# Seven blocks instead of eight in the second layer's mixture of experts

## The chip, the cores and the metric

The program runs on one core of one Trainium2 chip. The metric is the device time of one execution in microseconds (us), as the median of three runs. An execution takes about a thousandth of a second. In this text TensorE is called PE and its weight loads PEld, VectorE is DVE, ScalarE is ACT, GpSimd is POOL, and SyncE, whose queue issues most of the transfers, is SP.

## What is computed

Two layers over 256 latent tokens and 256 context tokens, width 1024, all in float32. Each layer has a mixer (attention) and a mixture of 16 experts, of which each token uses two. The change lies in the second layer's mixture, where only the 256 latent tokens are left. It is this much of the reference:

```python
expert_id = g_idx[:, None] * EXPERTS_PER_GROUP + top_i
dense_gate = jnp.einsum('nk,nke->en', weights, jax.nn.one_hot(expert_id, N_EXPERTS, dtype=jnp.float32))

def expert_step(acc, params):
    wg, wu, wd, gate = params
    y = (jax.nn.silu(tok @ wg) * (tok @ wu)) @ wd
    return acc + gate[:, None].astype(y.dtype) * y, None

out, _ = lax.scan(expert_step, jnp.zeros_like(tok), (w_gate, w_up, w_down, dense_gate))
```

`wg` and `wu` are 1024 x 512, `wd` is 512 x 1024: 6 MiB for an expert, 96 MiB for the layer. After the mixture comes a last RMSNorm.

## The kernel before

The kernel does not compute every expert for every token. It gathers for each expert the tokens that chose it into **slots**, a fixed number for each (`CAPS`, L32). In the second layer the first four experts by number (ranks 12 to 15) have 32 slots each; the other twelve are ranked on the chip by how many tokens chose them, and ranks 0 and 1 have 192 slots, ranks 2 and 3 have 128, ranks 4 to 11 have 32. Tokens that find no slot go through a slow path behind a branch (L1752) that is entered only if there are any.

128 slots make a **block** (`PLAN` L37, `block_plan` L55). Of the second layer's eight blocks, block 0 holds the four experts with known numbers, 32 slots each (a "q" entry); blocks 1 and 2 one expert each, ranks 3 and 2 ("m"); the "w" entry makes three blocks: block 3 with the last 64 slots of ranks 0 and 1, and blocks 4 and 5 with their first 128; blocks 6 and 7 hold ranks 8 to 11 and 4 to 7.

Each block has three products: gate (G), up (U) and down (D). The string `TURNS` (L69) gives their order in the second layer by hand: G6 is the gate product of block 6. The rest of this text names products in that way. In a product, PE holds the block's tokens as weights and streams the expert's matrix through, 512 columns at a time, with one instruction of `T.matmul` for each tile of the block (L1658 for G and U, L1691 for D). Tiles of 32 or 64 slots lie side by side in the array's columns, so that a block of four 32-slot tiles takes four matmuls for what a block of one 128-slot tile does with one. This text calls one such pass of 512 columns a **round**: every product has 8 rounds, whatever its tiles. (The trace shows each matmul as two instructions.)

Around the products, each block costs PE some more work: `pick` (L1326), 48 short matmuls that gather the block's tokens out of three bf16 parts, at kt = 2 of the product ahead of its G; `ready` (L1427, L1430), which lays out the gather matrix and the gates; `a_turn` (L1619), four transposes between U and D; and `ship` with `chunk` (L1589, L1596), which spreads the block's result back over the tokens, eight matmuls put behind later products by `spread_some`.

The weights come in **loads** of 1 MiB (128 partitions x 8 KiB), two for each expert and product: the first half serves rounds 1 to 4, the second rounds 5 to 8. `Experts.todo` (L1003) lists all 96 loads of the layer in the order in which `TURNS` needs them first; this text numbers them 0 to 95. They rotate over 18 buffers (`more["order"]`, L1919), so load n has to wait until the last product that reads load n - 18 is done. All are issued on SP's queue, in order, at most eight under way: an issue that waits holds up all that stand behind it. The matrices of ranks 0 to 11 can be addressed only when the ranking is known; then SP reads each expert's number out of `perm` into a register (`value_load`, L1020) the first time that it is wanted. Loads 0 to 15 are issued earlier; `experts.issue(len(fixed) - 4 + 2 * l)` (L1349) issues what is left of the experts with known numbers ahead of the ranking.

Of the kernel before, what the change touches and what calls it, by code (L numbers as in the profile page):

```python
# [30 lines left out]

CAPS = (  # L32
    (192, 192) + (128,) * 4 + (64,) * 10,
    (192, 192) + (128,) * 2 + (32,) * 12,
)

PLAN = (  # L37
    (("p", 14, 15), ("m", 2), ("p", 12, 13), ("m", 3), ("p", 10, 11), ("w", 0, 1), ("m", 4), ("m", 5), ("p", 8, 9),
     ("p", 6, 7)),
    (("q", 12, 13, 14, 15), ("m", 3), ("m", 2), ("w", 0, 1), ("q", 8, 9, 10, 11), ("q", 4, 5, 6, 7)),  # L40
)
MAXSLOTS = max(sum(c) for c in CAPS)

# [1 line left out]
def bases(layer):  # L45

    out, n = [0] * NE, 0
    for _, *rs in PLAN[layer]:
        for r in rs:
            out[r] = n  # L50
            n += CAPS[layer][r]
    return out


def block_plan(layer):  # L55

    base, blocks = bases(layer), []
    for kind, *rs in PLAN[layer]:
        if kind == "w":
            pair = [(base[r] + 128, 64, r) for r in rs]  # L60
            ones = [[(base[r], 128, r)] for r in rs]
            blocks += [pair] + ones if layer else [ones[0], pair, ones[1]]
        else:
            blocks.append([(base[r], 128 // len(rs), r) for r in rs])
    return blocks

TURNS = ("G0 U0 G1 U1 D0 D1 G6 G4 U6 U4 G3 G5 D6 U3 D4 U5 D3 D5 G7 G2 U2 U7 D2 D7")  # L69


def products(layer):

    if layer:
        return [("GUD".index(t[0]), int(t[1:])) for t in TURNS.split()]
    out, n = [], len(block_plan(layer))
    for b in range(n):
        turn = [(0, b), (1, b)], [(2, b - 1)] * (b > 0)  # L80
        out += turn[1] + turn[0] if b == n - 1 else turn[0] + turn[1]
    return out + [(2, n - 1)]
# [83 lines left out]
def hybrid_kernel(ctx: ExitStack, tc: tile.TileContext, A: dict, dbg=None):  # L166
# [829 lines left out]
    class Experts:  # L996


        def __init__(self, l):
            self.l, self.w, self.regs, self.perm = l, {}, {}, None  # L1000
            blocks = block_plan(l)
            self.known = NE - NFIX[l]
            self.todo = list(dict.fromkeys((r, which, h) for which, b in products(l) for h in range(2)  # L1003
                                           for _, _, r in blocks[b]))
            if l == 0:
                self.todo.sort(key=lambda p: p[0] < self.known)
# [36 lines left out]
    def moe(l, ntb, experts, yp, yT, finish, w_o, place, after_loads):  # L1043
# [214 lines left out]
        fx = tl([ntb, nfix], "fx")  # L1258
        V.scalar_tensor_tensor(fx, pos[:, :, 0:nfix], 1.0, Mb[:, :, 0:nfix], op0=ALU.add, op1=ALU.mult)
        blocks = block_plan(l)  # L1260

        solo = [len(b) == 1 and l in SPLIT for b in blocks]
# [699 lines left out]
```

## Time and profile before

| what | value |
| --- | --- |
| time, median of three runs | 1064.69 us (1059.69 to 1064.75) |
| time of the profiled execution | 1066.53 us |
| its span, first to last instruction | 1064.7 us |
| busy in the span: PE, DVE, ACT | 985.5, 556.2, 397.3 us |
| mean granted clock of TensorE | 0.976 of 2.4 GHz |
| moved by DMA | 309.85 MB, mean 291 GB/s |
| second layer's products, first G0 to the end of D7 | 824.8 to 1049.6 us |

The profile gives busy time by engine, the rate of the DMA, the idle time of each engine with the engine that ended it, and the instructions in order of time. A busy PE can be a PE that waits inside a matmul, so the count of rounds in a stretch is read beside its busy share. The rows that the prediction uses stand below, in groups.

### The profile page before, as it was taken

The numbers are of one execution on the slowest core, as the hardware profiler recorded it, in microseconds if no ns is written. First come the engines' busy times: TensorE is split into PE (matmuls) and PEld (weight loads), VectorE is DVE, ScalarE is ACT, GpSimd is POOL, SyncE is SP. The second block draws the span as 40 slices with busy tenths as digits, with TensorE's granted clock in tenths as the row PEclk, the third lists the DMA queues.
The fourth block names the chain that finished last, engine by engine and source line by source line (L and its number), as shares of the span: only waits on it lengthen the run. The fifth ranks groups of instructions, "written<-read, shape, count | busy, mean of one in ns | idle before, by whom it ended". The sixth has DMA issues, their size and how long they took to land. (4 is left out here: it accounts for less than half of the span.)

```text
span 1064.7 us, 14592 instructions
## 1 busy us (share of the span) xinstructions
PE 985.5 (93%) x5205; PEld 574.6 (54%) x5205; DVE 556.2 (52%) x1354; ACT 397.3 (37%) x817; POOL 49.2 (5%) x73
## 2 busy tenths in 40 slices
PE   4899999897999989999986999998878999999995
PEld 3666555686555435566422668885556444434532
DVE  3564465767565545578325745627877422214324
ACT  4254343643234324567204525327873311100211
POOL 3000100100000000000021000000000000000000
PEclk9999999999999999999989999999998999999998
DMA  9988877536779998989896593333164999999991
GB/s 284 367 332 323 342 312 275 201 136 212 289 312 411 358 422 307 367 332 357 333 383 228 215 398 128 119 119 158 41 220 139 383 420 419 420 374 408 380 374 41
DMA packets 66950, 309.85 MB, mean 291 GB/s; under 512 B 6544, under 2 KB 14944, under 8 KB 37176
## 3 DMA queue, kind: packets, MB, share of 16 engines
q1 hardware_dynamic: 56408, 277.01, 67.0%
q0 software_dynamic: 5984, 19.26, 5.3%
q10 hardware_dynamic: 4480, 12.59, 3.3%
q8 instruction: 43, 0.70, 0.3%
q14 instruction: 35, 0.29, 0.1%
HBM read 299.85 MB, written 8.98 MB: 290 GB/s over the span
## 5 line engine op out<-in xcount | busy, mean ns | idle before, releaser
L1658 PE MATMUL gu<-we,xT 128*64 128x512 f32 (+1 forms) x512 | 119.6, 616 | 3.2 <-DMA we<-in_w_up_dram 3.2
L1691 PE MATMUL dn<-we,aT 128*64 128x512 f32 (+2 forms) x480 | 119.1, 606 | 2.8 <-DMA we<-in_w_down_dram 2.6
L317 ACT CAST wh<-we 128x512 fp32r<-128x512 f32 x144 | 85.5, 621 | 64.1 <-PE dn L322 24.3
L1658 PE MATMUL gu<-we,xt 128*32 128x512 f32 (+2 forms) x448 | 105.2, 596 | 0.0
L318 DVE TENSOR_TENSOR wl<-we,wh 128x512 fp32r<-128x512 f32 x144 | 92.2, 687 | 20.9 <-ACT wh L317 19.2
L321 PE MATMUL mm<-wh,hT 128*128 128x512 f32 x248 | 101.5, 409 | 1.8 <-ACT hT L317 1.8
L322 PE MATMUL mm<-wh,hT 128*128 128x512 f32 x248 | 97.8, 394 | 0.7 <-DVE hT L318 0.7
L323 PE MATMUL mm<-wl,hT 128*128 128x512 f32 x248 | 98.1, 395 | 0.0
L1691 PEld LDWEIGHTS dn<-we,aT 128*64 128x64 f32 (+2 forms) x480 | 36.0, 134 | 66.1 <-issue 59.1
L1658 PEld LDWEIGHTS gu<-we,xT 128*64 128x64 f32 (+1 forms) x512 | 33.7, 133 | 62.3 <-issue 54.6
L1658 PEld LDWEIGHTS gu<-we,xt 128*32 128x32 f32 (+2 forms) x448 | 36.3, 136 | 57.2 <-issue 55.1
L318 DVE TENSOR_TENSOR wl<-wi,wh 128x512 fp32r<-128x512 f32 x52 | 35.7, 690 | 48.3 <-ACT wh L317 34.6
L1669 DVE TENSOR_TENSOR sg<-sg,gu 128x256 f32<-128x256 f32 x40 | 15.2, 417 | 83.8 <-PE gu L1658 80.8
L321 PEld LDWEIGHTS mm<-wh,hT 128*128 128x128 f32 x248 | 46.9, 189 | 20.5 <-issue 8.4
L317 ACT CAST wh<-wi 128x512 fp32r<-128x512 f32 x52 | 32.1, 621 | 64.0 <-PE mm L322 59.6
L323 PEld LDWEIGHTS mm<-wl,hT 128*128 128x128 f32 x248 | 46.9, 189 | 12.2 <-issue 0.8
L322 PEld LDWEIGHTS mm<-wh,hT 128*128 128x128 f32 x248 | 47.0, 189 | 10.6 <-DVE hT L318 1.0
L317 ACT CAST y<-y 128x512 fp32r<-128x512 f32 x16 | 9.9, 618 | 97.6 <-DVE y L1589 85.1
L321 PE MATMUL mm<-wo,yT 128*128 128x512 f32 x96 | 40.9, 426 | 2.3 <-ACT wo L317 2.3
L350 PE MATMUL ada<-wada,cs 128*32 128x512 f32 x320 | 40.8, 600 | 0.5 <-DMA wada<-in_w_ada_dram 0.5
L1664 ACT ACTIVATE sg<-gu 128x512 f32<-128x512 f32 x20 | 11.9, 597 | 77.7 <-PE gu L1658 72.0
L323 PE MATMUL mm<-lo,yT 128*128 128x512 f32 x96 | 39.2, 410 | 1.1 <-DVE lo L318 1.0
(367 smaller groups left out, 1658.0 us busy)
## 6 DMA issues: line engine op xcount, KB each, us to landing
we<-in_w_gate_dram SPq DMA_DIRECT2D x64, 1024.0 KB, 10.3
we<-in_w_up_dram SPq DMA_DIRECT2D x62, 1024.0 KB, 8.7
we<-in_w_down_dram SPq DMA_DIRECT2D x60, 1024.0 KB, 15.9
wada<-in_w_ada_dram SPq DMA_DIRECT2D x48, 1024.0 KB, 8.9
wi<-in_w_in_odd_dram SPq DMA_DIRECT2D x12, 1024.0 KB, 8.9
win<-in_w_in_even_dram SPq DMA_DIRECT2D x4, 1024.0 KB, 11.7
wo<-in_w_out_even_dram SPq DMA_DIRECT2D x4, 1024.0 KB, 8.3
we<-in_w_down_dram ACTq DMA_DIRECT2D x4, 1024.0 KB, 14.7
```

The costliest lines, as they stand in the source:

```text
L317: S.copy(hi, src)
L318: V.tensor_tensor(out=lo, in0=src, in1=hi.bitcast(F32), op=ALU.subtract)
L321: T.matmul(ps, a[0], b[0], start=start, stop=False)
L322: T.matmul(ps, a[1], b[0], start=False, stop=False)
L323: T.matmul(ps, a[0], b[1], start=False, stop=stop)
L350: T.matmul(ps[32 * j:32 * j + 32], cs[:, kt, :], part(w, k)[:, 512 * j:512 * j + 512], start=(kt == 0), stop=(kt == KT - 1))
L1658: T.matmul(ps[c:c + n_], xTs[bi][0][:, kt, c:c + n_], part(experts.w[r, which], kt), start=(kt == 0), stop=(kt == KT - 1))
L1664: S.activation(parted(sgs[bi], 4), by_part(ps, 4), AF.Silu)
L1669: V.tensor_tensor(out=sg[:, c], in0=sg[:, c], in1=up[:, c], op=ALU.mult)
L1691: T.matmul(ps[h][c:c + n_], aTs[bi][0][:, f, c:c + n_], part(experts.w[r, 2], f)[:, 512 * h:512 * h + 512], start=(f == 0), stop=(f == 3))
```

## The change

`CAPS` gives ranks 0 and 1 160 slots in the second layer (192 before) and rank 3 64 (128 before). A new "x" entry takes the place of rank 3's "m" and of the "w" entry. It makes three blocks: ranks 0 and 1 with 128 slots each, and one block of four tiles of 32 slots: the last 32 of rank 0, the last 32 of rank 1, and two tiles of rank 3. Seven blocks are left: 0 (ranks 12 to 15), 1 (rank 2), 2 (rank 0), 3 (rank 1), 4 (the four tiles), 5 (ranks 8 to 11), 6 (ranks 4 to 7). `TURNS` is written anew for them. The branch of "x" for four ranks is not taken here.

```diff
@@ -31,13 +31,14 @@
 CAPS = (
     (192, 192) + (128,) * 4 + (64,) * 10,
-    (192, 192) + (128,) * 2 + (32,) * 12,
+    (160, 160) + (128, 64) + (32,) * 12,
 )
 PLAN = (
     ...
-    (("q", 12, 13, 14, 15), ("m", 3), ("m", 2), ("w", 0, 1), ("q", 8, 9, 10, 11), ("q", 4, 5, 6, 7)),
+    (("q", 12, 13, 14, 15), ("m", 2), ("x", 0, 1, 3), ("q", 8, 9, 10, 11), ("q", 4, 5, 6, 7)),
 )
@@ -60,13 +61,19 @@
+        elif kind == "x":
+            ones = [[(base[r], 128, r)] for r in rs[:2]]
+            tiles = lambda *rs: [(base[r] + n, 32, r) for r in rs for n in range(128 if CAPS[layer][r] > 128 else 0,
+                                                                                CAPS[layer][r], 32)]
+            blocks += ones + [tiles(*rs)] if len(rs) == 3 else [ones[0], tiles(rs[0], rs[2]), ones[1],
+                                                                tiles(rs[1], rs[3])]
         else:
             blocks.append([(base[r], 128 // len(rs), r) for r in rs])
-TURNS = ("G0 U0 G1 U1 D0 D1 G6 G4 U6 U4 G3 G5 D6 U3 D4 U5 D3 D5 G7 G2 U2 U7 D2 D7")
+TURNS = ("G0 U0 D0 G2 U2 G4 U4 D2 G3 U3 D4 D3 G6 U6 G1 G5 U1 D6 U5 D1 D5")
```

The order moves in two places of which the prediction speaks. Lines of the changed kernel stand 7 higher (L1658 is L1665, L1691 is L1698, L1596 is L1603, L1619 is L1626, L1020 is L1027, L216 is L223).

The first is SP's queue where the ranking becomes known. `perm` is the ranking; `we` is a buffer of weights. Before, SP reads one number behind the first sixteen loads and goes on with a gate matrix:

```order
L216 DMA we<-in_w_up_dram 128x2048 x8
L1020 TENSOR_LOAD perm
L1020 ISA x2
L216 ISA
L216 DMA we<-in_w_gate_dram 128x2048
L216 ISA
L216 DMA we<-in_w_gate_dram 128x2048
L216 ISA
L216 DMA we<-in_w_up_dram 128x2048
L216 ISA
L216 DMA we<-in_w_up_dram 128x2048
L216 DMA we<-in_w_down_dram 128x2048 x8
```

In the changed kernel two of block 0's eight down loads stand ahead of the first read:

```order
L223 DMA we<-in_w_gate_dram 128x2048 x8
L223 DMA we<-in_w_up_dram 128x2048 x8
L223 DMA we<-in_w_down_dram 128x2048 x2
L1027 TENSOR_LOAD perm
L1027 ISA x2
```

Ten reads follow in a row; the last two of them, and what stands behind:

```order
L1027 TENSOR_LOAD perm
L1027 ISA x2
L1027 TENSOR_LOAD perm
L1027 ISA x2
L223 DMA we<-in_w_down_dram 128x2048 x6
L223 ISA
L223 DMA we<-in_w_gate_dram 128x2048
```

What moved: block 0's down loads go from places 20 to 27 of the list to places 16 to 23, and ten reads of the ranks, of which one stood there and the others singly between later loads, stand in front of load 18.

The second is the end of PE's program. `gu` and `dn` are the products' sums, `xt` the gathered tokens, `aT` the turned activations, `sp` the spreading. Before, from U2 on (U2, U7, D2, the start of D7):

```order
L1658 MATMUL gu<-we,xt 128x512 x8
L1658 MATMUL gu<-we,xt 32x512 x16
L1619 MATMUL tr<-cst,sg 128x128 x4
L1658 MATMUL gu<-we,xt 32x512 x16
L1691 MATMUL dn<-we,aT 128x512 x4
L1619 MATMUL tr<-cst,sg 128x128 x4
L1691 MATMUL dn<-we,aT 128x512 x4
L1691 MATMUL dn<-we,aT 32x512 x2
```

In the changed kernel, from U5 on (the rest of U5, D1, the start of D5):

```order
L1665 MATMUL gu<-we,xt 32x512 x31
L1698 MATMUL dn<-we,aT 128x512 x4
L1626 MATMUL tr<-cst,sg 128x128 x4
L1698 MATMUL dn<-we,aT 128x512 x4
L1698 MATMUL dn<-we,aT 32x512 x2
```

The last three products are now U5, D1 and D5, which need 18 loads that no earlier product reads; before they were U7, D2 and D7, which needed 18 as well, behind G7, G2 and U2 with 12. What follows the last D is the same list of instructions in both.

## Rows read from the trace of the kernel before

**Rows 1.** Page, part 2: rate of the DMA in 40 slices of 26.6 us.

```profile
GB/s 284 367 332 323 342 312 275 201 136 212 289 312 411 358 422 307 367 332 357 333 383 228 215 398 128 119 119 158 41 220 139 383 420 419 420 374 408 380 374 41
```

**Rows 2.** Stretches of the second mixture: busy us (count) by engine, PE's clock, DMA.

```profile
825.00:830.00 5.00, 5.00 (x52) 1.49 (x48) 5.00 (x12) 3.43 (x4) 0.00 (x0) 1.00 0.73 239
830.00:930.00 100.00, 98.36 (x684) 44.52 (x678) 28.75 (x107) 14.95 (x27) 0.00 (x0) 1.00 1.01 418
930.00:1035.00 105.00, 104.36 (x535) 45.29 (x532) 28.97 (x56) 11.80 (x20) 0.00 (x0) 1.00 0.97 395
1035.00:1050.00 15.00, 14.63 (x76) 4.77 (x75) 6.12 (x9) 1.59 (x3) 0.00 (x0) 1.00 0.02 9
1050.00:1064.70 14.70, 2.67 (x8) 1.42 (x8) 8.00 (x15) 4.01 (x12) 0.00 (x0) 0.78 0.20 73
...
950.00:960.00 10.00, 9.47 (x39) 4.00 (x40) 4.05 (x7) 1.09 (x2) 0.00 (x0) 1.00 0.75 264
```

**Rows 3.** PE's groups by shape, 820 to 1060 us: xcount | busy, mean ns.

```profile
L1658 PE MATMUL gu<-we,xt 128*128 128x512 f32 x128 | 56.8, 596 | 0.0
L1326 PE MATMUL pick<-pick,h 128*128 128x128 bf16 x336 | 21.0, 219 | 1.5 <-DVE pick L1419 1.5
L1596 PE MATMUL sp<-y,hot 128*128 128x512 f32 x64 | 20.1, 440 | 2.6 <-ACT y L317 2.3 <-DVE y L318 0.2
L1658 PE MATMUL gu<-we,xt 128*64 128x512 f32 x64 | 15.7, 599 | 0.0
L1691 PE MATMUL dn<-we,aT 128*64 128x512 f32 x32 | 7.3, 598 | 0.0
L1619 PE MATMUL tr<-cst,sg 128*128 128x128 f32 x32 | 5.0, 279 | 0.0
...
L1427 PE MATMUL hot<-identb,pick 128*128 128x128 bf16 x16 | 2.4, 221 | 0.1
```

**Rows 4.** What SP's queue waited for, 820 to 1060 us: total, times, longest.

```profile
SPq L216 <- PE gu L1658: 46.9, 15, 16.2
...
SPq L1020 <- DVE base L1369: 14.2, 1, 14.2
```

**Rows 5.** SP's reads of the ranks, 822 to 854 us: ns, first and last start.

```profile
L1020 SPq TENSOR_LOAD <-perm x5: 267/270/453, 823.9 to 853.3; - x5
L1020 SPq FUSED_REGOPS  x5: 152/152/162, 824.5 to 853.6; - x5
L1020 SPq SEQ_ASSERT  x5: 18/18/18, 824.7 to 853.8; - x5
```

**Rows 6.** SP's issues of loads 16 to 19 in order of time: start, us.

```profile
825.11 1.78 SPq L216 DMA_DIRECT2D we<-in_w_gate_dram  x2
828.41 0.91 SPq L216 DMA_DIRECT2D we<-in_w_up_dram  x2
```

**Rows 7.** PE in order of time, first block, one broken round, and D7.

```profile
824.76 7.07 PE L1658 MATMUL gu<-we,xT 128*32 128x512 f32 x64
...
835.19 2.85 PE L1326 MATMUL pick<-pick,h 128*128 128x128 bf16 x48
...
838.16 5.36 PE L1658 MATMUL gu<-we,xT 128*32 128x512 f32 x48
...
883.01 1.05 PE L1658 MATMUL gu<-we,xt 128*32 128x512 f32 x2
...
1042.55 7.08 PE L1691 MATMUL dn<-we,aT 128*32 128x512 f32 x56
```

**Rows 8.** End of the first layer's mixture: PE in order of time, idle before it.

```profile
539.63 3.65 PE L1658 MATMUL gu<-we,xT 128*64 128x512 f32 x14
...
547.54 6.35 PE L1658 MATMUL gu<-we,xT 128*64 128x512 f32 x14 [2.16 <-DMA we<-in_w_up_dram]
...
562.62 5.34 PE L1691 MATMUL dn<-we,aT 128*64 128x512 f32 x14 [2.63 <-DMA we<-in_w_down_dram]
```

**Rows 9.** One microsecond after the wait of 2.16: PE busy, PE's clock, DMA.

```profile
550.00:551.00 1.00, 1.00 (x4) 0.50 0.99 414
```

## Prediction

> **What bounds the kernel now.** I read the views in this order: the rates by slice, then the stretches of the second mixture, then its groups by shape, then SP's waits, then the two queues in order of time. The rate of the DMA [rows 1] shows where the change can act: from slice 31, at 825 us, to slice 38 it stays at 374 to 420 GB/s, while earlier slices fall to 41. That is the second mixture, and there two things are full at once [rows 2]. From 830 to 930 us PE is busy for 98.36 of 100 us at full clock, and the DMA engines are busy too, at 418 GB/s; from 930 to 1035 us PE has 104.36 of 105 us and the DMA 395 GB/s, with a hole of which 950 to 960 us shows most (264 GB/s). The order of ending tells which of the two is the bound: the DMA falls to nothing from 1035 us on, and PE goes on alone until D7 ends at 1042.55 + 7.08 = 1049.6 us [rows 7]. PE is the bound by some 15 us, and the loads follow close behind, held back at times by PE itself, which has not yet freed a buffer (46.9 us of SP's waits [rows 4], most of them covered by the eight loads under way). After D7 come 15.1 us of spreading, norm and output, up to 1064.7.
>
> One 128-slot block takes 56.8 / 4 = 14.2 us for G and U, so 0.888 us for each of the 64 rounds [rows 3]; a block of four 32-slot tiles has the same G in 7.07 us [rows 7]. One load takes 1.049 MB / 418 GB/s = 2.5 us.
>
> **The change part by part.** *A block less.* Taken from the old block 3: G and U 15.7, D 7.3, its pick 21.0 / 7 = 3.0, its spreading 20.1 / 8 = 2.5, its turn 5.0 / 8 = 0.6, its `hot` 0.3 [rows 3]: 29.4 us of PE. With nothing else in the way, D5 would end at 1049.6 - 29.4 = 1020.2 us.
>
> *The loads are not fewer.* All 96 are still read. So the floor is set by them. Before, load 16 was issued at 825.11 us, when the ranking was known, and load 18 at 828.41 us, when G0 had freed its first buffers [rows 6]. In the changed kernel loads 16 and 17 need no ranking; they can go as soon as their memory is free, in a time in which the queue sat for 14.2 us waiting for the ranking [rows 4]. That saves two loads, 5 us, of the busy stretch. Against it, load 18 now stands behind ten reads of the ranks. One takes from 853.3 to 853.8 us and a little [rows 5], I take 0.6; the first starts at 823.9 [rows 5], so load 18 goes at 830.3 us instead of 828.4. Bounds: 0.44 us each by the three durations alone (829), 0.8 by the first, longer one (832). From issue to full rate I take 1.7 us: 825 to 830 us moved 239 x 5 = 1.2 MB [rows 2], 2.8 us' worth. Loads 18 to 95 then take 78 x 2.5 = 195 us, up to 1027.0 us, if no buffer is ever late. That is 8 us earlier than now, and already 7 us later than PE would be done. The bound passes from PE to the DMA.
>
> *Which buffer is late.* Load n takes the place of load n - 18. By the new order the tightest pair is load 56, of G6 and U6, behind load 38, the first half of rank 1's down matrix, which is last read in rounds 1 to 4 of D3. When is that? U0 ended at 838.16 + 5.36 = 843.5 us with block 1's pick (2.85) and `hot` in it [rows 7]; without these, 840.3. From there to the middle of D3 stand D0, G2, U2, G4, U4, D2, G3, U3, D4 and half of D3: 76 rounds, 67.5 us; four picks, 12.0; four `hot`, 1.2; four turns, 2.5; 16 spreading matmuls, 5.0 [rows 3]. In sum 88.2. Two things are added for which the trace of before has only neighbours: D0 follows U0 directly, so its turn waits for DVE in the open (0 to 2 us), and in U4 the picks break a block's round of four tiles twice, where one broken piece took 1.05 us against the 0.22 of a quarter [rows 7] (0 to 1.7). I take 1.5 for both: half of D3 is done at 930.0, load 56 begins at 931.7. Without the stall it would have begun at 832.0 + 38 x 2.5 = 927.0, so the hole is 4.7 us. The 40 loads from 56 on end at 931.7 + 100 = 1031.7 us, and by then PE has been waiting for them: its work up to D6, which precedes U5, D1 and D5, is done before U5's loads are in (1006.7).
>
> *What remains behind the last load.* D5's last four rounds need it: half of 7.08 is 3.5 us, and 0.5 from landing to start. These rounds follow a wait, and the end of the first layer shows what such waits do to PE: behind waits for a load of 2.16 and 2.63 us, fourteen instructions took 6.35 and 5.34 us, where 3.65 is usual [rows 8], at the lower clock of 1.2 GHz, half of the granted [rows 9]. I take the smaller loss, 1.7 us, since the stretch that waits is short; bounds 0 and 3.5. Then the tail, which is the same list of instructions, 15.1.
>
> *Sum:* 1031.7 + 0.5 + 3.5 + 1.7 + 15.1 = 1052.5, against a span of 1064.7: 12.2 us less. The profiled execution took 1066.53, 1.8 more than the median of the runs (1064.69), and would give 1054.3; the median gives 1052.5. I predict **1053 us**. DVE and ACT lose a block's work too and stay far under PE (28.75 and 14.95 us of 100 [rows 2]); that is worth nothing.
>
> **Rivals.** *No buffer is late.* If half of D3 is done by 925 us, the loads run through: 1027.0 + 0.5 + 3.5 + 1.7 + 15.1 = 1048, or 1046 without the clock's loss. For it: before, PE fitted the same kinds of pieces with little idle. Against it: the sum above has no slack of 5 us in it.
>
> *D3 comes late.* Each of the four picks ahead of D3 waits for DVE as the worst one did before (of the 1.5 us there [rows 3], most was one wait), 4.4 us, and the two unknowns above come out at their upper ends, 2.2 more: load 56 begins at 938, and the end is 1059 to 1060. Against it: all seven picks together waited 1.5 us.
>
> *The clock stays low* (slower than before). From the last of U5's loads on, at 1006.7 us, PE has 4 + 8 + 4 + 4 rounds and 8 spreading matmuls ahead of it. If the granted clock is half throughout, as behind the waits of the first layer, these take 20 x 1.78 + 5.0 = 40.6 us, to 1047.3; a slower tail makes it 1064, and the same at D0, which also waits for its loads, moves D3 by up to 5 us: 1069. The trace speaks for the mechanism [rows 8, 9], but for one group of instructions behind each wait, not for a whole stage. It decides from the point at which D5's first half ends later than the last load lands. The Trainium skill (TensorE: Matmul & The Clock Gate, section "Loop structure matters more than you think") states it as a rule against such an order: matmuls that each wait for their DMA run at the lower clock. By that rule the sum would be the rival's, 1064 to 1069; by the rows here, 1.7 us.
>
> *The change doesn't do what it says.* If more tokens than slots chose an expert, the branch behind the mixture would be entered, with six loads and 48 rounds at least for one expert: 15 + 42 us, some 1110. Counting the choices out of the reference's inputs, I find 141, 127, 70 and 56 tokens for ranks 0 to 3 (160, 160, 128, 64 slots), 27 for rank 4 and 9 at most for the known four (32 each). It should not happen.
>
> **How the numbers follow.** Chances: forecast 0.60 (1049 to 1058), no buffer late 0.14, D3 late 0.14, low clock 0.10, branch 0.02. 0.5%, about what a measurement of this kernel can tell from no change, is 5.3 us here, so the bounds are 1059.4 and 1070. Faster: 0.58 of the forecast, the 0.14, and 0.06 of the late D3, 0.78. Slower: the branch and 0.04 of the low clock, 0.06. The rest, 0.16, is no change. The range reaches down to the rival without a late buffer (1046, with 1 us for the reads' lower bound) and up through the late D3 (1060, with 2 us of the clock's loss): 1045 to 1062, which leaves out most of the low clock, the branch and the tails.
>
> **What would show it.** Right: loads 16 and 17 issued ahead of the first read, load 18 near 830 us; the DMA full from 832 us with one hole of 3 to 6 us near 930; from U5 on PE waits for `we`, and the last load lands near 1032; D5 ends near 1037, and 15 us follow. Wrong: the DMA's end earlier than PE's by over 8 us (PE is still the bound); several holes in the DMA (the buffers' order is worse than I see); a granted clock of 0.5 over most of 1007 to 1037.

## The result, and the profile after

The changed kernel takes 1047.47 us (median of four executions, 1046.94 to 1048.10), the kernel before in the same comparison 1064.72, so the medians lie 17.25 us apart. The ratio, which here and below is estimated from the single executions and is not the quotient of the two medians, is 0.9852, 95% interval 0.983 to 0.9874. The profiled execution took 1046.94 us, its span 1044.3. Repeated later beside the kernel before, the changed kernel had 1049.25 against 1065.88, ratio 0.9855 (0.9828 to 0.9881).

The rate of the DMA from the page (part 2, 40 slices of 26.1 us) answers [rows 1]:

```profile
GB/s 282 365 301 309 347 317 315 148 226 146 282 357 367 384 389 375 347 295 356 366 356 303 274 307 192 154 115 202 1 159 216 270 418 419 421 400 419 420 421 126
```

The last eight slices lie in the second mixture. Before, four slices there stood at or above 400; now seven in a row do, and there is no slice of 374 or 380 any more. The stretches by time (columns as in [rows 2]) show where the full rate begins and ends:

```profile
819.09:825.00 5.91, 5.91 (x57) 1.84 (x60) 5.88 (x16) 3.88 (x5) 0.00 (x0) 1.00 0.02 4
825.00:830.00 5.00, 4.88 (x44) 1.39 (x40) 3.79 (x31) 3.14 (x4) 0.00 (x0) 1.00 0.94 347
830.00:923.00 93.00, 92.14 (x640) 43.32 (x631) 25.84 (x70) 11.28 (x21) 0.00 (x0) 1.00 1.01 420
923.00:925.00 2.00, 2.00 (x6) 0.86 (x5) 0.75 (x1) 0.00 (x0) 0.00 (x0) 1.00 0.96 348
925.00:929.00 4.00, 4.00 (x29) 1.90 (x31) 3.40 (x6) 0.62 (x1) 0.00 (x0) 1.00 1.02 424
929.00:933.00 4.00, 4.00 (x44) 1.29 (x40) 1.13 (x2) 0.62 (x1) 0.00 (x0) 1.00 0.92 326
933.00:1020.00 87.00, 79.86 (x487) 31.00 (x480) 19.46 (x40) 8.83 (x15) 0.00 (x0) 1.00 1.01 420
...
1023.00:1024.00 1.00, 0.71 (x2) 0.25 (x3) 0.00 (x0) 0.00 (x0) 0.00 (x0) 1.00 0.46 184
1024.00:1025.00 1.00, 1.00 (x3) 0.11 (x1) 0.00 (x0) 0.00 (x0) 0.00 (x0) 1.00 0.23 94
1025.00:1026.00 1.00, 0.40 (x5) 0.17 (x8) 0.00 (x0) 0.00 (x0) 0.00 (x0) 1.00 0.05 20
```

The DMA now runs at 420 GB/s almost from end to end, and PE is the one that pauses: 79.86 busy of 87 us from 933 on, against 104.36 of 105 in [rows 2]. The hole of 950 to 960 us is gone; a small one is left from 923 to 933, where (420 - 348) x 2 + (420 - 326) x 4 = 520 KB are missing, 1.2 us at 420 GB/s.

PE in order of time, G0, the turn into D0, D3, G6, and then what follows D6 (idle time before a group in brackets, with what ended it) answers [rows 7]:

```profile
819.09 7.07 PE L1665 MATMUL gu<-we,xT 128*32 128x512 f32 x64
...
836.33 1.92 PE L1698 MATMUL dn<-we,aT 128*32 128x512 f32 x16 [0.19 <-DVE aT L1632]
...
919.67 5.40 PE L1698 MATMUL dn<-we,aT 128*128 128x512 f32 x12
...
926.85 7.08 PE L1665 MATMUL gu<-we,xt 128*32 128x512 f32 x64
...
990.92 3.63 PE L1665 MATMUL gu<-we,xt 128*32 128x512 f32 x28 [1.02 <-DMA we<-in_w_up_dram]
995.92 1.05 PE L1665 MATMUL gu<-we,xt 128*32 128x512 f32 x2 [1.37 <-DMA we<-in_w_up_dram]
998.41 1.04 PE L1665 MATMUL gu<-we,xt 128*32 128x512 f32 x2 [1.45 <-DMA we<-in_w_up_dram]
1000.89 3.62 PE L1665 MATMUL gu<-we,xt 128*32 128x512 f32 x26 [1.44 <-DMA we<-in_w_up_dram]
...
1023.29 1.90 PE L1698 MATMUL dn<-we,aT 128*32 128x512 f32 x4 [0.59 <-DMA we<-in_w_down_dram]
1025.79 3.62 PE L1698 MATMUL dn<-we,aT 128*32 128x512 f32 x20 [0.60 <-DMA we<-in_w_down_dram]
```

From U5 on PE waits for `we`, 5.3 us in U5 and 1.2 in D5; before, no product waited there. The last load releases PE at 1025.79 us, and D5 ends at 1029.41.

The groups by shape, 820 to 1045 us, answer [rows 3]: G and U of 128-slot blocks have 96 instructions instead of 128, those of 64-slot tiles are gone.

```profile
L1665 PE MATMUL gu<-we,xt 128*128 128x512 f32 x96 | 42.8, 596 | 0.0
L1698 PE MATMUL dn<-we,aT 128*128 128x512 f32 x48 | 22.0, 600 | 0.0
L1333 PE MATMUL pick<-pick,h 128*128 128x128 bf16 x288 | 17.8, 219 | 0.0
```

SP's wait for the ranking, which was 14.2 us in [rows 4] (total, times, longest):

```profile
SPq L1027 <- DVE base L1376: 7.0, 1, 7.0
```

Its ten reads, which answer [rows 5] (ns, first and last start):

```profile
L1027 SPq TENSOR_LOAD <-perm x10: 262/265/461, 818.3 to 823.6; - x10
```

Its issues of block 0's down loads and the two behind them, which answer [rows 6] (start, us):

```profile
810.78 16.67 SPq L223 DMA_DIRECT2D we<-in_w_down_dram  x8
827.73 0.95 SPq L223 DMA_DIRECT2D we<-in_w_gate_dram  x2
```

Loads 16 and 17 go ahead of the first read, at 810.78 us and after; their data are through before 819 us, and the DMA then stands still until 825 us (4 GB/s above), while SP reads ranks.

The hole has two parts. From 923 to 925 us 144 KB are missing, behind load 56, which waits for the first half of D3: that is done at 921.4, and SP's next issue starts at 921.66. From 929 to 933 us 376 KB are missing, 0.9 of the 1.2 us: load 60 takes the place of load 42, which is last read in the first half of G6, and G6 follows D3 with only spreading in between. SP's wait for it (total, times, longest), and the issue that followed (start, us), from 929 to 931 us:

```profile
SPq L223 <- PE gu L1665: 5.0, 1, 5.0
...
930.50 0.33 SPq L223 DMA_DIRECT2D we<-in_w_gate_dram  x1
```

**A marker.** In these two traces G0 starts at 824.76 and 819.09 us, 5.7 us apart, although PE has the same instructions up to there. So times below are counted from G0's start, and the stretch from it to the end of the span is the one to compare: 239.9 us before, 225.2 after, 14.7 less.

### The profile page after: what moved, and what is told of

It is laid out like the page before. It is cut to its first block, busy times and chain, and to the rows that moved or that the text cites. A ratio compares the mean times of both kernels' runs of the same rounds, so it can differ in the third digit from the quotient of the medians.

```text
span 1044.3 us, 14537 instructions
## 1 busy us (share of the span) xinstructions
PE 960.4 (92%) x5187; PEld 560.2 (54%) x5187; DVE 548.1 (52%) x1334; ACT 394.0 (38%) x811; POOL 49.5 (5%) x73
## 5 line engine op out<-in xcount | busy, mean ns | idle before, releaser
L1665 PE MATMUL gu<-we,xT 128*64 128x512 f32 (+1 forms) x512 | 117.0, 611 | 1.9 <-DMA we<-in_w_up_dram 1.9
L1698 PE MATMUL dn<-we,aT 128*32 128x512 f32 (+2 forms) x496 | 112.5, 598 | 4.3 <-DMA we<-in_w_down_dram 4.0
L1665 PE MATMUL gu<-we,xt 128*32 128x512 f32 (+1 forms) x480 | 95.0, 596 | 5.3 <-DMA we<-in_w_up_dram 5.3
L1698 PEld LDWEIGHTS dn<-we,aT 128*32 128x32 f32 (+2 forms) x496 | 34.3, 127 | 64.3 <-issue 51.6
L1665 PEld LDWEIGHTS gu<-we,xT 128*64 128x64 f32 (+1 forms) x512 | 33.5, 133 | 59.5 <-issue 53.8
L1665 PEld LDWEIGHTS gu<-we,xt 128*32 128x32 f32 (+1 forms) x480 | 30.5, 125 | 56.6 <-issue 45.8
L330 PEld LDWEIGHTS mm<-wl,hT 128*128 128x128 f32 x248 | 47.1, 190 | 12.2 <-DVE wl L325 0.8
L329 PEld LDWEIGHTS mm<-wh,hT 128*128 128x128 f32 x248 | 47.2, 190 | 10.7 <-DVE hT L325 0.9
L328 PE MATMUL gu<-wh,xT 128*128 128x512 f32 x96 | 39.1, 408 | 0.8 <-ACT wh L324 0.8
## 6 DMA issues: line engine op xcount, KB each, us to landing
win<-in_w_in_even_dram SPq DMA_DIRECT2D x4, 1024.0 KB, 10.9
we<-in_w_down_dram ACTq DMA_DIRECT2D x4, 1024.0 KB, 14.9
```

The costliest lines, as they stand in the source:

```text
L328: T.matmul(ps, a[0], b[0], start=start, stop=False)
L329: T.matmul(ps, a[1], b[0], start=False, stop=False)
L330: T.matmul(ps, a[0], b[1], start=False, stop=stop)
L1665: T.matmul(ps[c:c + n_], xTs[bi][0][:, kt, c:c + n_], part(experts.w[r, which], kt), start=(kt == 0), stop=(kt == KT - 1))
L1698: T.matmul(ps[h][c:c + n_], aTs[bi][0][:, f, c:c + n_], part(experts.w[r, 2], f)[:, 512 * h:512 * h + 512], start=(f == 0), stop=(f == 3))
```

## The experiments

All numbers of this table are read from the traces of the runs told below; the last three columns are counted from G0's start.

| kernel | G0 starts, us | D3 resumes | last load releases PE | end of span |
| --- | --- | --- | --- | --- |
| before; again | 824.76; 824.66 | | | 239.9; 240.8 |
| changed; again | 819.09; 819.49 | 100.6; 100.4 | 206.7; 205.0 | 225.2; 223.4 |
| changed, spare PE work late | 824.43 | 100.7 | 206.7 | 225.1 |
| changed, spare PE work early | 825.71 | 107.3 | 211.7 | 230.1 |
| changed, reads behind the loads; again | 821.22; 822.26 | 100.2; 100.4 | 204.6; 205.2 | 223.0; 224.3 |
| changed, reads doubled (in vain) | 821.67 | 100.4 | 206.0 | 225.1 |
| changed, two loads less, early | 822.62 | 99.2 | 203.8 | 222.3 |
| changed, two loads less, late | 823.69 | 100.7 | 201.5 | 220.0 |
| before, spare PE work late | 821.70 | | | 246.0 |
| before, D0 and D1 early | 825.36 | | | 237.8 |
| seven blocks, old order | 825.06 | | 212.4 | 231.7 |

("D3 resumes" is the start of the last 12 of its 16 instructions; D3's half is 4 of these, some 1.75 us, later.)

**Both kernels once more.**

> The kernel before once more, unchanged. In the two traces at hand G0 of the second mixture starts at 824.8 us (before) and 819.1 us (after), although PE has the same instructions up to there. Theory: this is a difference between executions, in the time ahead of the change, and the loads ahead of G0 make it. Then G0 can start near 819 here too, and the stretch from G0's start to the end stays at 239.9 us whatever G0's start. Rival: the change itself brings G0 forward (for instance by the earlier issue of loads 16 and 17); then G0 starts near 824.8 here again.

> The changed kernel once more, unchanged. In the traces so far G0 of the second mixture starts anywhere from 819.1 to 825.7 us, and what lies behind that start is the same to some tenths where PE's program is the same. Theory: from G0's start to the end of the span 225.2 us again, with D5's last wait ending at 206.7 us behind G0's start; the median lies some 16 us below the kernel before (ratio 0.985). Rival: the 225.2 us of the first trace were a lucky execution; then this one shows several us more.

The start of G0 differs from execution to execution in either kernel: over the fourteen traces it lies anywhere from 819.1 to 825.7 us. The kernel before again had 824.66, which by itself fits the rival of that run; what speaks against the rival are the changed kernel and its variants, which with the same instructions of PE up to G0 have 819.1, 819.5, 824.4 and 825.7, among others. A part of the spread is seen in the six matmuls of `warm` (twelve instructions) ahead of G0, PE in order of time. The changed kernel:

```profile
810.01 2.84 PE L243 MATMUL warm<-cst 128*128 128x256 f32 x12
```

The changed kernel with spare work behind U1, far later:

```profile
814.84 4.36 PE L243 MATMUL warm<-cst 128*128 128x256 f32 x12
```

The kernel before again:

```profile
813.95 5.47 PE L236 MATMUL warm<-cst 128*128 128x256 f32 x12
```

In the first the granted clock is 1.00 from 809.59 to 817.09 us; in the second it is 0.80 on average over the same 7.5 us counted from G0, in the third 0.68. That is worth 1.6 us at most: from the start of `warm` to G0 9.1, 9.6 and 10.7 us pass in the three. `warm` itself starts anywhere from 810.0 to 815.6 us in the fourteen traces, so most of the spread arises further ahead, where it was not taken apart. Since the changed kernel can start G0 as late as the kernel before, the 5.7 us of the two traces at hand are not counted as its gain; that about 1 us of them belongs to the change is not excluded. From G0 on the rival of a lucky trace falls: the second trace of the changed kernel had 223.4, not several us more than the first but 1.8 less. The expectation of 225.2 again failed by the same 1.8, nearly all of it in the landing of the last load (205.0 against the 206.7 expected).

**More PE work, late and early.**

```diff
-                    T.matmul(ps[c:c + n_], ...)
+                    done = T.matmul(ps[c:c + n_], ...)
+            if l and (which, bi) == (1, 1):      # late: behind U1; early: (1, 4); in the kernel before: (1, 2)
+                warm(16, done)
```

> The changed kernel with 16 spare matmuls (a constant, 256 columns, result unused) behind U1, ahead of D6: some 6.9 us more work of PE in the last third. Theory (the loads are the bound there: PE waits 6.5 us for them in U5 and D5): the waits take it up, 0 to +1 us. Rival (PE is still the bound, its waits are only shifted work): +6.9 us.

> The changed kernel with the same 16 spare matmuls behind U4, ahead of D2, G3, U3, D4 and D3: 6.9 us more work of PE before the product that sets load 56's buffer free. Theory (load 56 waits for D3's half): the hole in the loads at that place grows by about the same and the end moves by +5.5 to +6.9 us, although PE's total is that of the run with the spare work late. Rival (the stream of loads has slack at that place): 0 to +2 us.

> The kernel before with the same 16 spare matmuls (some 6.9 us of PE) behind U2, in its last stretch. Theory (PE is the bound of the kernel before by some 15 us): +6.5 to +7 us, the full amount. Rival (the loads bound it already): 0 to +2 us.

Late, 7.07 us of PE cost nothing: 225.1 us, and the ratio to the kernel before is 0.9838 (0.9814 to 0.9863), that of the changed kernel. The spare work, the one wait that is left in U5, and D5:

```profile
980.22 7.07 PE L243 MATMUL warm<-cst 128*128 128x256 f32 x32
...
1006.22 3.62 PE L1665 MATMUL gu<-we,xt 128*32 128x512 f32 x26 [0.26 <-DMA we<-in_w_up_dram]
...
1031.12 3.62 PE L1700 MATMUL dn<-we,aT 128*32 128x512 f32 x20 [0.59 <-DMA we<-in_w_down_dram]
```

U5's waits of 5.3 us have shrunk to 0.26; D5's are as they were. The loads set the end, and PE has some 5 us to spare there.

Early, the same work costs 4.9 us (230.1 against 225.2; 6.7 against the second trace), and the median 1056.95 against 1064.64 of the kernel before (0.9912, 0.9886 to 0.9938). The theory stands in this: at this place PE counts. But the hole is not where I had put it. Three stretches of this run:

```profile
905.00:910.00 5.00, 5.00 (x13) 2.21 (x12) 2.16 (x4) 1.24 (x2) 0.00 (x0) 1.00 0.25 49
...
932.00:937.00 5.00, 5.00 (x33) 2.85 (x31) 1.39 (x7) 1.15 (x3) 0.00 (x0) 1.00 0.84 293
...
943.00:947.00 4.00, 4.00 (x43) 1.04 (x32) 0.69 (x1) 0.47 (x1) 0.00 (x0) 1.00 0.84 281
```

From 905 to 910 us the DMA moves 49 GB/s: 4.4 us are missing there, and 2.8 at the two later places that answer to the two parts of the changed kernel's hole. At 905 us G3 begins. Counting the list of loads, load 46 takes the place of load 28, rank 1's gate matrix, which G3 is the last to read. In the changed kernel nothing is missing at that place (420 GB/s from 830 to 923 us). Here G3 begins 6.8 us later behind G0's start (79.2 against 72.5 us) and 4.4 are lost, so by this estimate the pair had some 2.4 us to spare there. It is nearly as tight as load 56 behind load 38, and it is met first when PE comes late.

The kernel before pays for nearly all of it: D7 starts 5.4 us later (1044.89 - 821.70 = 223.2, against 217.8 from [rows 7]), the end comes 5.2 to 6.1 us later, and the ratio is 1.0073 (1.005 to 1.0095). I had expected 6.5 to 7; the medians lie 7.5 us apart, and why the traces show a little less was not taken apart. PE was the bound there, as read.

**The start of the loads.**

```diff
+        more["sent"] = d      # in load(): the DMA that was issued last
...
+                    if self.l and self.fixed_sent is not None:
+                        with tc.issue_after(self.fixed_sent.ins):    # block 0's last load is issued first
+                            self.regs[by, r] = by.value_load(self.perm[0:1, r:r + 1], ...)
...
+            if r >= self.known:
+                self.fixed_sent = more["sent"]
```

> The changed kernel with the ten reads of the ranks put behind block 0's six remaining down loads on SP's queue, so that load 18 waits only for G0's first buffers (3.5 us behind G0's start instead of 5.1). Theory of the prediction (load 56 waits for D3's half, so a start that is earlier by 1.6 us only widens the hole at load 56): no change, 0 to -0.5 us. Rival (the stream of loads from 18 on is the bound from end to end, since the hole measured only some 1.4 us): -1.6 us. A third (D0 waits for load 16 to 23's first ones and PE comes earlier too): D3's half moves as well, about -1 us.

> The kernel with the ten reads behind block 0's loads once more, beside the changed kernel on the same chip. Its first trace had 223.0 us from G0's start to the end, 2.2 less than the changed kernel, with a hole at load 56 that was about 1 us wider. Theory (the last of the sixteen DMA engines sets the landing of the last loads, and it has no hole): 222.5 to 223.5 us again, and a median 1 to 3 us below the changed kernel's. Rival (the first trace's 2.2 us were chance): 225.

Load 18 is issued 3.7 us behind G0's start instead of 5.1. The rates around D3 in the first of the two traces:

```profile
923.00:925.00 2.00, 2.00 (x6) 0.80 (x6) 0.03 (x1) 0.00 (x0) 0.00 (x0) 1.00 0.76 262
925.00:931.00 6.00, 6.00 (x37) 2.86 (x39) 4.37 (x7) 0.62 (x1) 0.00 (x0) 1.00 0.98 389
931.00:935.00 4.00, 4.00 (x40) 1.17 (x36) 0.91 (x2) 0.62 (x1) 0.00 (x0) 1.00 0.89 297
```

Missing to 420 GB/s are (158 x 2 + 31 x 6 + 123 x 4) = 994 KB, 2.4 us instead of 1.2: of the time won at the start, most is given back in the hole, as the theory says. The end lay 2.2 us lower in the first trace, 0.9 in the second (against 225.2), close to the spread of the changed kernel's own traces (223.4 to 225.2), and the medians on one chip are alike: 1049.18 and 1049.25 us. The first trace by itself goes beyond the rival's 1.6 us less, which the second and the medians do not bear out; the expectation of the second run (222.5 to 223.5, and a lower median) failed. A gain under 1 us is not excluded; a better kernel it is not.

> The changed kernel with each rank read twice in the second layer (the second value is used, the first is not), so that twenty reads stand ahead of load 18, which goes some 5.8 us later. It doubles the one wait that the change adds. Theory (the stream of loads from 18 on is the bound but for the hole of some 1.3 us at load 56): +4 to +5.8 us. Rival (D3's half sets load 56, so that a later start is hidden in the hole): 0 to +2 us.

This one missed its aim. The second reads went into SP's queue between later loads; ten reads stand ahead of load 18 as before, and it is issued 5.1 us behind G0's start. It is a third trace of the changed kernel: 225.1 us.

```diff
         self.todo = list(dict.fromkeys((r, which, h) ...))
+        self.skip = [(12, 2, 1), (13, 2, 1)] if l else []     # late: (8, 0, 1), (9, 0, 1)
+        self.todo = [p for p in self.todo if p not in self.skip]
...
-            self.w.setdefault((r, which), []).append(w)
+            self.w.setdefault((r, which), []).extend([w] * (1 + ((r, which, 1) in self.skip)))
```

> The changed kernel with two loads left out near the start of the stream: the second halves of the down matrices of the first two experts with known numbers (block 0) are not read, and rounds 5 to 8 of D0 use the first halves in their place. PE has the same rounds (the planner swaps a few pieces of spreading and picking), the DMA 2 loads or 5.0 us less. Theory (load 56 waits for D3's half): the time is not won, the hole at that load grows from some 1.3 to some 6 us; 0 to -2 us from G0's start to the end (225.2, 223.4 us in the two traces of the changed kernel). Rival (the stream of loads is the bound from end to end): -5 us.

> The changed kernel with two loads left out behind the hole: the second halves of the gate matrices of ranks 8 and 9 (block 5) are not read, and rounds 5 to 8 of their tiles use the first halves. PE's program is the same instruction by instruction. Theory (from load 56 on the loads are the bound, and PE waits some 6.5 us for them in U5 and D5): -4 to -5 us from G0's start to the end. Rival (PE is the bound there): 0 to -1 us.

These two tell it best. Late, 5.0 us of loads less give 5.2 us against the first trace and 3.4 against the second; the ratio to the kernel before falls to 0.9788 (0.977 to 0.9806). Early, the same 5.0 us give 2.9 and 1.1, and the ratio, 0.9844 (0.9821 to 0.9867), is that of the changed kernel. Both ran on one chip, and their medians, 1043.93 late and 1048.79 early, lie 4.9 us apart. D3 itself came 1.4 us earlier there (the program lays out the pieces of picking and spreading by a plan of its own, and some changed places), so of the loads' 5.0 us at most 1.5 are won beyond that. Where the rest went, ahead of D3's half and behind it:

```profile
896.00:924.00 28.00, 28.00 (x167) 13.31 (x166) 9.07 (x21) 3.90 (x7) 0.00 (x0) 1.00 0.98 389
924.00:928.00 4.00, 4.00 (x12) 2.08 (x11) 1.00 (x2) 0.00 (x0) 0.00 (x0) 1.00 0.98 389
928.00:932.00 4.00, 4.00 (x33) 1.50 (x35) 3.58 (x6) 0.97 (x2) 0.00 (x0) 1.00 0.93 324
932.00:936.00 4.00, 4.00 (x40) 1.04 (x32) 0.69 (x1) 0.27 (x1) 0.00 (x0) 1.00 0.76 262
```

Up to 924 us 868 KB are missing, 2.1 us, and behind it 1140 KB, 2.7 us, most of them from 932 us on, where load 60 waits for G6. That is 4.8 us of holes against 1.2 in the changed kernel, so 3.6 of the 5.0 us went there. Up to D3 and the first half of G6 PE releases the buffers and sets the pace, and from there the loads do.

**Block and order apart.**

```diff
-TURNS = ("G0 U0 G1 U1 D0 D1 G6 ...")
+TURNS = ("G0 U0 D0 G1 U1 D1 G6 ...")      # eight blocks, the rest as before
```

> The kernel before, with its eight blocks, and one edit of its order: D0 directly behind U0, D1 behind U1. So loads 16 and 17 need no ranking, as in the changed kernel, and the reads of the ranks stand in a row ahead of load 18. It isolates the change of the loads' start. Theory (PE is the bound): the loads run earlier, PE's end does not move: -1 to +1 us. Rival (the earlier start of the loads is itself a gain of the change): -3 to -5 us.

2.1 to 3.0 us less than before in the traces (ratio of the times 0.9983, 0.9964 to 1.0002), between the two expectations. But it is no gain of the loads. The stretch of 232 instructions of PE from G6's start on, in the kernel before:

```profile
879.36:910.96 31.60, 30.09 (x232) 13.63 (x231) 7.64 (x22) 4.28 (x8) 0.00 (x0) 1.00 1.01 419
```

The same 232 in this one:

```profile
880.65:909.34 28.69, 28.69 (x232) 13.57 (x231) 6.69 (x20) 4.47 (x8) 0.00 (x0) 1.00 1.01 419
```

2.9 us less, of which 1.5 are idle time of PE ahead of the picks, which waited for DVE in the kernel before (the 1.5 of [rows 3]); with D1 moved, no pick waits there. The other 1.4 us lie in PE's busy time (30.09 against 28.69). The DMA has 419 GB/s in both.

```diff
-TURNS = ("G0 U0 D0 G2 U2 G4 U4 D2 G3 U3 D4 D3 G6 U6 G1 G5 U1 D6 U5 D1 D5")
+TURNS = ("G0 U0 G1 U1 D0 D1 G5 G2 U5 U2 G4 G3 D5 U4 D2 U3 D4 D3 G6 U6 D6")
```

> The changed kernel's seven blocks in an order like that of before: G0 U0 G1 U1 D0 D1, then blocks 5, 2, 4, 3, and 6 last. So loads 16 and 17 are rank 2's and wait for the ranking again, one read stands ahead of them, and the last products are G6, U6 and D6 with 24 loads. It isolates the block that is gone from the order. Theory (the loads are the bound once PE has a block less, and this order holds them up at more places): some 3.5 us slower than the changed kernel, 13 to 14 us faster than before. Rival (the new order is worth nothing): as the changed kernel. Rival (the new order makes most of the gain): within 5 us of before.

8.2 us less than before, 6.5 more than the changed kernel (ratio to before 0.9935, 0.9909 to 0.9961): between the first expectation and the last, and met by none. So the order is worth nearly as much as the block, taken in this sequence; eight blocks in the new order were not run. Its stretches:

```profile
835.06:945.06 110.00, 108.49 (x730) 47.75 (x726) 24.38 (x75) 12.69 (x24) 0.00 (x0) 1.00 1.01 420
945.06:965.06 20.00, 18.36 (x124) 6.22 (x119) 6.12 (x10) 1.24 (x2) 0.00 (x0) 1.00 0.69 262
965.06:1034.00 68.94, 64.81 (x366) 24.79 (x364) 20.00 (x35) 7.33 (x12) 0.00 (x0) 0.95 1.01 420
```

The hole is (420 - 262) x 20 / 420 = 7.5 us instead of 1.2; the last load releases PE 5.7 us later than in the changed kernel.

## Why the prediction was right, and where its terms were off

The forecast was 1053 us, the result 1047.5; the range (1045 to 1062) and the sign held. The mechanism is shown: the bound passed from PE to the loads (spare work late costs nothing, loads left out late count fully), and ahead of that, around G3, D3 and G6, PE holds the stream up (spare work early costs, loads left out early count little). Two things were off. The time lies below the stretch that the forecast itself was given (1049 to 1058) and beside the rival "No buffer is late" (1046 to 1048); it is in the range because the lower end was taken from that rival. And the hole was smaller than forecast and for the most part at another load. Step by step, from G0's start (824.76 in the prediction's frame):

| step | predicted | changed kernel; again |
| --- | --- | --- |
| load 18 is issued | 5.5 | 5.1; 5.1 |
| U0 ends | 15.5 | 15.6 |
| D3's half is done | 105.2 | 102.3; 102.2 |
| hole in the loads | 4.7 | 1.2 |
| last load releases PE | 207.4 | 206.7; 205.0 |
| loss by a low clock behind it | 1.7 | 0; 0 |
| rest of D5 | 3.5 | 3.6; 3.6 |
| tail | 15.1 | 14.9; 14.8 |
| end of the span | 227.7 | 225.2; 223.4 |

**What failed first was the sum up to D3's half.** A round was taken as 0.888 us, from the busy time of a group divided by its rounds; but groups of matmuls overlap at their ends (D3's group of 5.40 us from 919.67 on would end at 925.07, and the next one starts at 924.50), so busy times add up to more than the time that passes. From U0's end at 834.73 to D3's half at 921.4 us 86.7 us pass. Taking each other group by the time until the next one starts, 10.9 of them are picks, 1.0 `hot`, 5.5 spreading and 3.2 turns with their waits; 66.1 are left for 76 rounds, 0.87 each. Against the working, the rounds are 1.4 less, the picks 1.1, `hot`, turns and the two unknowns together 1.0; the spreading is 0.5 more. The hole shrinks with it, though not by this alone: D3's half 2.9 us earlier and load 18 0.4 us earlier leave 4.7 - 2.9 + 0.4 = 2.2 us by the prediction's own working, and 1.2 were measured. Of these only 0.3 stand behind load 56; 0.9 stand behind load 60, a wait that the prediction does not have. The rival "No buffer is late" wanted D3's half by 925 us in the old frame, 100.2, and it came at 102.3. The truth lay between forecast and rival, and the time on the rival's side.

**Against it went a term that I did not have.** From D3's half to the release by the last load I had 102.2 us; the three traces show 104.4, 102.8 and 103.8. The last rows of the stretches above say why: the rate falls over three microseconds, to 184, 94 and 20 GB/s. These three rows moved 298 KB, 0.7 us' worth at 420 GB/s, in the 2.8 us up to the release: 2.1 us where the sum has 0.5. 420 GB/s over 16 engines is 26 each, so at the end about one engine is still at work. On that reading the load has landed when the last of them is through. In the second trace the fall is shorter:

```profile
1022.00:1023.00 1.00, 1.00 (x3) 0.30 (x4) 0.00 (x0) 0.00 (x0) 0.00 (x0) 1.00 1.01 414
1023.00:1024.00 1.00, 0.85 (x2) 0.00 (x0) 0.00 (x0) 0.00 (x0) 0.00 (x0) 1.00 0.60 242
1024.00:1025.00 1.00, 0.55 (x8) 0.26 (x9) 0.00 (x0) 0.00 (x0) 0.00 (x0) 1.00 0.30 119
```

There the last load released PE 1.7 us earlier. That single engines lag is read from the rates alone; no run took it apart. Differences of under 2 us between the ends of two single traces are therefore not read as effects here.

**The clock's loss was put at the wrong place.** 1.7 us were taken behind the last load; D5's second half took 3.62 us in every trace of the changed kernel and its variants. The mechanism exists, one product earlier, and not in every execution. In the first trace the clock stays at 1.00 through U5's waits of 1.02 to 1.45 us; in the second, with waits of up to 1.45 us as well, it falls, and the same 26 instructions take 5.33 us instead of 3.62:

```profile
997.06 1.92 PE L1665 MATMUL gu<-we,xt 128*32 128x512 f32 x2 [1.45 <-DMA we<-in_w_up_dram]
999.54 5.33 PE L1665 MATMUL gu<-we,xt 128*32 128x512 f32 x26 [0.57 <-DMA we<-in_w_up_dram]
```

```profile
995.00:999.00 4.00, 2.52 (x4) 0.18 (x2) 0.00 (x0) 0.00 (x0) 0.00 (x0) 0.65 1.02 424
999.00:1002.00 3.00, 2.46 (x12) 0.59 (x16) 0.00 (x0) 0.00 (x0) 0.00 (x0) 0.50 1.00 415
```

The 1.7 us are lost in U5 and found again in D5, whose loads are not there yet: that trace is the faster of the two. Over the changed kernel and its variants the 26 instructions took 3.62 us in four traces and 4.07 to 5.74 in five. The low-clock rival did not come. The Trainium skill (TensorE: Matmul & The Clock Gate, section "Loop structure matters more than you think") has it that matmuls with a long wait for a DMA between every two of them go to the lower clock. The waits here are at most 1.45 us; the second trace agrees for some 7 us, the first not at all.

**The median.** 1064.7 - 1047.5 = 17.2, of which my 12.2 explain the larger part; the stage itself lost 14.7 us in the first pair of traces, and 15.8 by the means (240.4 before, 224.6 over the changed kernel's three traces). The remainder is no more than what the time ahead of G0 varies.

**The other steps.** Loads 16 and 17 ahead of the reads, ten reads in a row at 0.59 us each (818.3 to 823.6 for nine of them), the turn into D0 in the open, PE's waits from U5 on, and the tail came as written. One sentence holds only in part: that load 56 is *the* tightest pair. The larger part of the hole stands behind load 60, and load 46 behind G3 is close.

## What to carry to other kernels

When work is taken from the bounding engine, its gain ends at the next floor: here 29.4 us of PE were removed by the working and some 15.8 came out, because the loads stood that close behind. Where loads rotate through buffers, list for each load the product that frees its place: here a microsecond of loads saved behind the last such place counted fully or nearly so, and one saved ahead of it hardly counted. And count from a marker inside the program when the executions differ ahead of the stage that was changed.

## What the runs showed of the hardware that I had not expected

- The same instructions ahead of G0 ran at the full or at the lower clock from one execution to the next: `warm` took 2.84 us in some (granted clock 1.00) and up to 5.47 in others (0.68 over 7.5 us). That is up to 1.6 us of the 6.6 over which G0's start spread.
- A stream of loads did not end at full rate: the rate fell over up to three microseconds (184, 94 and 20 GB/s), as if the sixteen DMA engines did not end together, and the last landing of one and the same program varied by 1.7 us.
- Ten reads of a number into a register on SP's queue took 5.9 us in which no load was issued (the first starts at 818.3, load 18 goes at 824.2), and moving them away let load 18 go only 1.4 us earlier, since it then waited for G0's first buffers (3.7 us behind G0's start instead of 5.1).
